# A two-layer hybrid trunk on one core: attention's query blocks first to last, values block by block, output projection in another order, squares summed on ScalarE

## The chip, the core and the metric

The kernel runs on one core of a Trainium2 chip. The core has TensorE (PE in the profile; PEld is its loading of weights), VectorE (DVE), ScalarE (ACT), GpSimd (POOL) and SyncE (SP), which issues most DMA transfers. Each engine works through its own list of instructions in order; semaphores hold an instruction until what it needs is there. Matmuls write to PSUM, eight banks of 128 x 512 floats; all else lies in SBUF. The metric is the time of one execution on the device in microseconds (us).

## The reference: what is computed

The input is one sequence of 512 tokens of width 1024, float32. Two layers follow one another, each of them:

```python
x = x + 0.5 * swiglu(rms_norm(x, ffn1_norm[l]), ...)            # d_ff 2816
h = rms_norm(x, mix_norm[l])
a, g, q, k, v = jnp.split(h @ w_in[l], splits, axis=-1)          # each 512 wide
conv_out = conv_module(a, g, ...)     # a * sigmoid(g), causal depthwise conv of 31 taps, RMSNorm, SiLU
diff_out = diff_attention(q, k, v, ...)
x = x + jnp.concatenate([conv_out, diff_out], axis=-1) @ w_out[l]
x = x + 0.5 * swiglu(rms_norm(x, ffn2_norm[l]), ...)
```

The differential attention has 4 heads. Of each head two causal softmax maps are made (keys of width 64, with a relative-position bias); the first minus lambda times the second multiplies the values of width 128. The result of each head is normalised by its root mean square over the 128 values of a token.

## The kernel before

The activations lie transposed, features on partitions and tokens along the row: `x` is 8 tiles of 128 x 512. Large products are done as three matmuls of a high and a low part (`mm3`, lines 159, 162 and 163): high by high, low by high, high by low. The parts of the weights are made on the chip: `chunk` (line 99) loads 128 x 1024 floats by a DMA on SP's queue, ScalarE makes the high part (line 96), and VectorE or GpSimd subtracts to get the low part (line 97). These tiles come from rings: five raw buffers, four for high and four for low parts, and a buffer is given back when its last reader is done.

A layer is a feed-forward block, the mixer and another feed-forward block. The change touches the mixer alone (function `mixer`, lines 526 to 815). Its work in program order:

- `conv_in` projects the convolution's input in four channel groups; `project` gives q and k for two pairs of token blocks of 128, `to_features` transposes them to features (`qz`, `kt`). q and k of blocks 0 and 1 come in the first pair.
- `project_values(j)` gives the values of token block j: 24 matmuls of 512 columns into a bank with the tag "mm", then a copy with a scale (line 614).
- `conv_taps(c, n)` does the 31 taps of channel group c. Group 0 is done on GpSimd (products by ScalarE, line 652, sums by GpSimd, line 653), groups 1 and 2 on VectorE in a PSUM bank (lines 660 and 665), group 3 with ten taps on GpSimd and 21 on VectorE. `conv_finish` gathers the statistics, spreads them over the partitions (`rcv`), and makes the four finished tiles `ch`, `cl` (lines 675 to 684).
- Attention runs in 16 steps, a query block i of 128 tokens and a head h each. `softmaxes` makes the scores of both maps in a bank of the tag "sc" and one of "po" (two banks each), adds the bias and finds the row's extremum (line 703), takes the exponential with a row sum (line 707), and combines the maps (lines 710 to 713). `keys_first` transposes the combined map and copies it, `values` multiplies by the values into a bank of "mm" (`pos[i]`), and after head 3 of a block normalises all four heads at once: square on ScalarE (738), sum on VectorE (740), power on GpSimd (`rsqrt`), product on VectorE (744). `block_out` transposes the block back and writes its high and low parts into `ch`, `cl` (lines 756 to 761). The row of a step grows with the block: block i has (i + 1) x 128 keys. `attend(n)` issues the softmax of step n, the transposes of step n - 2, the values of n - 3 and, where a block is complete, its output at n - 5.
- The output projection takes 4 tiles of the conv half (`half` 0) or of the attention half (`half` 1) for each of 8 output tiles; its products go to banks of "sc" and "po" in turn and are added to `x` by VectorE (line 810). It ends with `after(m)`, which makes the next block's input parts and squares (`Prep.tile`, lines 249 to 260).

Before the change attention takes the last query block first. The value projections stand between the first two steps, all conv taps before the third. The three passes of the output projection are the conv half for all tokens, the attention half for the last 256 tokens and the attention half for the first 256 tokens. The last two use the same weight chunks, which are loaded once for both.

Program order is not the order on the engines. The kernel is written in a framework with a planner, which simulates the program with costs of its own (`schedule_with_timeline_sim=True`, line 912): whenever an engine comes free in that simulation, the planner takes the earliest instruction in program order whose inputs and buffers are ready. The list of each engine is then fixed; on the chip an instruction that comes late holds up those behind it. Only where the code says `keep_in_program_order` is an order kept; none of these places is touched.

Of the kernel before, what the change touches and what calls it, by code (L numbers as in the profile page):

```python
# [11 lines left out]
F32 = mybir.dt.float32  # L12
F32R = mybir.dt.float32r
I32 = mybir.dt.int32
AF = mybir.ActivationFunctionType
ALU = mybir.AluOpType
AX = mybir.AxisListType

P = 128
DEPTH = 2  # L20
SEQ = 512
DM = 1024
KT = DM // P
NT = SEQ // P
# [4 lines left out]
CT = CC // P  # L29
TAPS = 31  # L30
PAD = TAPS - 1
HEADS = 4
HD = 64
VD = 2 * HD
# [14 lines left out]
POOL_TAPS = (TAPS, 0, 0, 10)  # L49
# [17 lines left out]
def trunk(ctx: ExitStack, tc: tile.TileContext, xt, par, lamv, relb, onehot,  # L67
          gu1, dn1, wag, wqkv, wout, gu2, dn2, out):
    nc = tc.nc
    V, S, G, T = nc.vector, nc.scalar, nc.gpsimd, nc.tensor  # L70

    const = ctx.enter_context(tc.tile_pool(name="const", bufs=1))
    small = ctx.enter_context(tc.tile_pool(name="small", bufs=2))
    act = ctx.enter_context(tc.tile_pool(name="act", bufs=1))
    wp = ctx.enter_context(tc.tile_pool(name="wp", bufs=1))
    tmp = ctx.enter_context(tc.tile_pool(name="tmp", bufs=2))
# [3 lines left out]
    def f32(ap):  # L80
        return ap.bitcast(F32)
# [3 lines left out]
    def bank(tag, name):  # L85
        return psum.tile([P, 512], F32, tag=tag, name=name, bufs=BANKS[tag])
# [12 lines left out]
    def chunk(src, eng=None):  # L99
        raw, hi, lo = ring("wraw"), ring("whi"), ring("wlo")  # L100
        nc.sync.dma_start(raw, src)
        parts_of(raw, hi, lo, eng)
        return hi, lo
# [74 lines left out]
    for half in range(2):  # L178
        h, kk = slice(half * 512, (half + 1) * 512), range(half * KT // 2, (half + 1) * KT // 2)
# [21 lines left out]
    def rsqrt(v, n, use=""):  # L201
        y = small.tile([P, n], F32, tag=f"rs_y{n}{use}", name="rs_y")
        G.tensor_tensor(y, v, mhalf[:, :n], op=ALU.pow)
        return y
# [60 lines left out]
    def wpart(w, b, n=P):  # L265
        return w[0][:, b * n : (b + 1) * n], w[1][:, b * n : (b + 1) * n]
# [223 lines left out]
    nlam, gq, gsub, ghalf = [], [], [], []  # L490
# [35 lines left out]
    def mixer(l, pr, after):  # L526
        with tc.tile_pool(name="mix", bufs=1) as mp, tc.tile_pool(name="mt", bufs=2) as mt:
# [74 lines left out]
            def project_values(j):  # L602

                if 2 not in wts:
                    wts[2] = [chunk(wqkv[l, 2, kc], G) for kc in range(KT // 2)]
                t = slice(j * P, (j + 1) * P)
                ps = bank("mm", "ps_v")
                for k in range(KT):
                    wh, wl = wpart(wts[2][k // 2], k % 2, 512)
                    xh, xl = pr[k]  # L610
                    T.matmul(ps, xh[:, t], wh, start=k == 0, stop=False)  # L611
                    T.matmul(ps, xh[:, t], wl, start=False, stop=False)
                    T.matmul(ps, xl[:, t], wh, start=False, stop=k == KT - 1)
                S.activation(vv[:, j].rearrange("p h d -> p (h d)"), ps, AF.Copy, scale=row["c"][:, j : j + 1])
# [59 lines left out]
            def conv_finish():  # L674
                rcv = spread(rows_rstd(csum, CC, "c")[0], "rb")
                for c in range(CT):
                    z = ys[c]
                    hg = ghalf[l][:, c : c + 1]
                    G.tensor_tensor(z, z, rcv, op=ALU.mult)
                    th = mt.tile([P, SEQ], F32, tag="gl", name="th", bufs=1)  # L680
                    S.activation(th, z, AF.Tanh, scale=hg)
                    V.scalar_tensor_tensor(z, th, 1.0, z, op0=ALU.add, op1=ALU.mult)
                    S.activation(ch[:, c, :], z, AF.Copy, scale=hg)
                    V.scalar_tensor_tensor(cl[:, c, :], z, hg, f32(ch[:, c, :]), op0=ALU.mult, op1=ALU.subtract)


            steps = [(i, h) for i in reversed(range(NT)) for h in range(HEADS)]
            sums, pos, maps, ats = {}, {}, {}, {}

            def softmaxes(i, h):  # L690
                W = (i + 1) * P
                tq = slice(i * P, W)
                if h == 0:
                    sums[i] = small.tile([P, 2, HEADS], F32, tag="sums", name="sums")
                scs = [bank(tag, "ps_sc")[:, :W] for tag in ("sc", "po")]
                e0 = mt.tile([P, SEQ], F32, tag="e0", name="e", bufs=4)[:, :W]
                sm = sums[i]
                for m in range(2):
                    T.matmul(scs[m], qz[:, m, h, tq], kt[:, h, :W], start=True, stop=True)  # L699

                for m, (sc, e) in enumerate(zip(scs, (e0, scs[1]))):
                    mn = small.tile([P, 1], F32, tag=f"mn{m}", name="mn")
                    V.tensor_tensor_reduce(
                        out=e, in0=sc, in1=row["bias"][:, h, SEQ - W :], scale=1.0, scalar=3e38,
                        op0=ALU.add, op1=ALU.min, accum_out=mn,
                    )
                    S.activation(e, e, AF.Exp, bias=mn, scale=-1.0, accum_out=sm[:, m, h : h + 1])

                r2 = small.tile([P, 1], F32, tag="r2", name="r2")
                V.reciprocal(r2, sm[:, 1, h : h + 1])  # L710
                c2 = small.tile([P, 1], F32, tag="c2", name="c2")
                V.tensor_scalar(c2, r2, nlam[l], sm[:, 0, h : h + 1], op0=ALU.mult, op1=ALU.mult)
                V.scalar_tensor_tensor(e0, scs[1], c2, e0, op0=ALU.mult, op1=ALU.add)
                maps[i, h] = e0

# [9 lines left out]
            def values(i, h):  # L725
                if h == 0:
                    pos[i] = bank("mm", "ps_o")
                for j in range(i + 1):
                    T.matmul(pos[i][:, h * VD : (h + 1) * VD], ats[i, h][:, j * P : (j + 1) * P], vv[:, j, h, :],
                             start=j == 0, stop=j == i)  # L730
                if h < HEADS - 1:
                    return
                po = pos[i]

                se = small.tile([P, HEADS], F32, tag="se", name="se")
                V.scalar_tensor_tensor(se, sums[i][:, 0, :], VD * EPS, sums[i][:, 0, :], op0=ALU.mult, op1=ALU.mult)
                sq = tmp.tile([P, SEQ], F32, tag="sq", name="sq")
                S.activation(sq, po, AF.Square)
                so = small.tile([P, HEADS], F32, tag="so", name="so")
                V.tensor_reduce(so, sq.rearrange("p (h d) -> p h d", h=HEADS), axis=AX.X, op=ALU.add)  # L740
                G.tensor_tensor(so, so, se, op=ALU.add)
                ro = rsqrt(so, HEADS)
                ov = mt.tile([P, HEADS, VD], F32, tag="ov", name="ov")
                V.tensor_tensor(
                    ov, po.rearrange("p (h d) -> p h d", h=HEADS),
                    ro.unsqueeze(2).broadcast_to([P, HEADS, VD]), op=ALU.mult,
                )
                outs[i] = ov
# [14 lines left out]
            def attend(n):  # L763
                if n < len(steps):
                    softmaxes(*steps[n])
                if 2 <= n < len(steps) + 2:
                    keys_first(*steps[n - 2])
                if 3 <= n < len(steps) + 3:
                    values(*steps[n - 3])
                if n >= 5 and steps[n - 5][1] == HEADS - 1:  # L770
                    block_out(steps[n - 5][0])
# [14 lines left out]
            row["bias"] = bias  # L786

            for n in range(2):
                attend(n)
                project_values(NT - 1 - 2 * n)  # L790
                project_values(NT - 2 - 2 * n)
            for c in range(CT):
                conv_taps(c, POOL_TAPS[c])
            for n in range(2, len(steps) + 5):
                attend(n)
            conv_finish()

            for half, t in ((0, slice(0, SEQ)), (1, slice(SEQ // 2, SEQ)), (1, slice(0, SEQ // 2))):  # L800
                if t.stop == SEQ:
                    w = [None] * 4
                for m in range(KT):
                    if w[m // 2] is None:
                        w[m // 2] = chunk(wout[l, half, m // 2], G)
                    ps = bank(("sc", "po")[m % 2], "ps_out")[:, : t.stop - t.start]
                    for kk in range(4):
                        k = half * 4 + kk
                        mm3(ps, wpart(w[m // 2], (m % 2) * 4 + kk), (ch[:, k, t], cl[:, k, t]), kk == 0, kk == 3)
                    V.tensor_tensor(x[:, m, t], ps, x[:, m, t], op=ALU.add)  # L810

                    if half == 1 and t.start == 0 and m < KT // 2:
                        after(m)
            for m in range(KT // 2, KT):
                after(m)
# [101 lines left out]
```

## Time and profile before

| | us |
|---|---|
| median of 3 runs | 1803.87 (1802.54 to 1804.24) |
| the profiled execution | 1804.31 |
| its span, first to last instruction | 1802.2 |
| busy: TensorE, VectorE, ScalarE, GpSimd | 1785.8, 1202.8, 880.0, 624.4 |
| first layer's mixer in the trace, about | 376 to 560 |
| second layer's mixer, about | 1268 to 1452 |

Times of the trace count from its first instruction. A line of a group names the line of the code, the engine, the operation, what it writes and reads, the shape and how often; then the busy time, the mean of one in ns, and the idle time of its engine before it with what ended it. A row of the windows gives for a stretch of time how long each engine was busy in it, with the number of instructions, then the clock granted to TensorE, the share of the DMA engines and their rate. A row of waits says which instruction of an engine waited for which, how long in total, how often, and the longest. Matmuls overlap, and their recorded length is longer than the distance from one start to the next; an engine that shows as busy may still run below its best.

### The profile page before, as it was taken

How to read it: one execution, taken by the hardware profiler on the slowest of the kernel's cores; microseconds unless marked ns; L12 is line 12 of the kernel's file. 1: busy time of each engine (PE TensorE's matmuls, PEld its weight loads, DVE VectorE, ACT ScalarE, POOL GpSimd, SP SyncE). 2: the span in 40 equal slices, each digit the busy share in tenths (PEclk: the TensorE clock that was granted, in tenths of full speed). 3: DMA queues.
4: the chain of work that ended last, by engine and by line, in shares of the span. 5: the costliest groups of instructions: out<-in, count | busy, mean ns of one | idle time of the engine just before them, and what ended most of it. 6: DMA issues, size and time to landing. Idle time of an engine off the chain costs nothing.

```text
span 1802.2 us, 27871 instructions
## 1 busy us (share of the span) xinstructions
PE 1785.8 (99%) x10692; PEld 1584.9 (88%) x10692; DVE 1202.8 (67%) x1854; ACT 880.0 (49%) x1448; POOL 624.4 (35%) x430
## 2 busy tenths in 40 slices
PE   8999999999999999999999999999999999999999
PEld 6799899888778889899888998998887888998997
DVE  6957556568867857557576674665788587574662
ACT  5446345445854436346434462554558354463551
POOL 3025123269942024133110331322797320241320
PEclk9999999999999999999999999999999999999999
DMA  6446456333212346556433564664231133564561
GB/s 232 117 128 190 137 146 180 115 107 93 72 43 86 109 114 174 165 125 184 125 94 104 137 193 106 169 171 129 71 108 57 47 103 97 146 177 134 152 169 54
DMA packets 106021, 228.05 MB, mean 127 GB/s; under 512 B 11575, under 2 KB 29254, under 8 KB 105888
## 3 DMA queue, kind: packets, MB, share of 16 engines
q1 hardware_dynamic: 86880, 190.88, 32.7%
q0 software_dynamic: 18720, 35.23, 11.9%
q8 instruction: 83, 1.36, 0.3%
q14 instruction: 50, 0.41, 0.1%
q10 hardware_dynamic: 288, 0.16, 0.0%
HBM read 224.12 MB, written 3.42 MB: 126 GB/s over the span
## 4 chain that ended last, share of the span: by engine, by line
PE 95%; DVE 2%; issue 1%; ACT 1%; ACTq 0%; DVEq 0%
PE ps_pair L369 36%; PE ps_d L159 9%; PE ps_d L163 9%; PE ps_d L162 9%; PE ps_pair L162 6%; PE ps_pair L163 6%; PE ps_pair L159 6%; PE ps_pair L581 2%; PE ps_pair L583 2%; PE ps_pair L582 2%; PE ps_out L159 1%; PE ps_out L162 1%; PE ps_sc L699 1%; PE ps_out L163 1%; DVE actl L252 1%; PE ps_v L611 1%
## 5 line engine op out<-in xcount | busy, mean ns | idle before, releaser
L96 ACT ACTIVATE whi<-wraw 128x512 fp32r<-128x512 f32 (+1 forms) x580 | 458.0, 813 | 656.4 <-PE ps_d L162 226.3
L97 DVE TENSOR_TENSOR wlo<-wraw,whi 128x512 fp32r<-128x512 f32 (+1 forms) x536 | 509.5, 973 | 191.3 <-ACT whi L96 186.8
L369 PE MATMUL ps_pair<-acth,wlo 128*128 128x256 f32 x1024 | 289.8, 283 | 0.0
L369 PE MATMUL ps_pair<-actl,whi 128*128 128x256 f32 x1024 | 289.8, 283 | 0.0
L369 PE MATMUL ps_pair<-acth,whi 128*128 128x256 f32 x1024 | 289.7, 283 | 0.0
L162 PE MATMUL ps_d<-hl,whi 128*128 128x512 f32 x704 | 274.0, 389 | 0.0
L163 PE MATMUL ps_d<-hh,wlo 128*128 128x512 f32 x704 | 272.7, 389 | 0.0
L159 PE MATMUL ps_d<-hh,whi 128*128 128x512 f32 x704 | 268.7, 389 | 0.0
L137 POOL DMA_DIRECT2D wraw<-in_gu x64 | 77.2, 1206 | 464.5 <-DMA wraw<-in_gu 239.5
L369 PE MATMUL ps_pair<-th,wlo 128*128 128x256 f32 x768 | 217.3, 283 | 0.0
L369 PE MATMUL ps_pair<-tl,whi 128*128 128x256 f32 x768 | 217.2, 283 | 0.0
L369 PE MATMUL ps_pair<-th,whi 128*128 128x256 f32 x768 | 217.2, 283 | 0.0
L159 PE MATMUL ps_pair<-acth,whi 128*128 128x512 f32 x512 | 201.4, 396 | 7.6 <-ACT whi L96 7.6
L162 PE MATMUL ps_pair<-actl,whi 128*128 128x512 f32 x512 | 200.6, 393 | 0.7 <-DVE actl L252 0.6
L163 PE MATMUL ps_pair<-acth,wlo 128*128 128x512 f32 x512 | 200.2, 392 | 0.0
L142 POOL TENSOR_TENSOR wraw<-wraw 128x512 f32<-128x512 f32 x64 | 89.0, 1391 | 314.0 <-DMA wraw<-in_gu 268.9
L369 PEld LDWEIGHTS ps_pair<-actl,whi 128*128 128x128 f32 x1024 | 196.6, 192 | 0.3
L369 PEld LDWEIGHTS ps_pair<-acth,whi 128*128 128x128 f32 x1024 | 196.6, 192 | 0.3
L369 PEld LDWEIGHTS ps_pair<-acth,wlo 128*128 128x128 f32 x1024 | 196.6, 192 | 0.0
L465 DVE SCALAR_TENSOR_TENSOR x<-ps_d,x 128x512 f32<-128x512 f32 x96 | 64.9, 688 | 196.4 <-PE ps_d L163 196.4
L163 PEld LDWEIGHTS ps_d<-hh,wlo 128*128 128x128 f32 x704 | 132.2, 188 | 27.0
L159 PEld LDWEIGHTS ps_d<-hh,whi 128*128 128x128 f32 x704 | 132.2, 188 | 26.9
(171 smaller groups left out, 3308.1 us busy)
## 6 DMA issues: line engine op xcount, KB each, us to landing
wraw<-in_gu SPq DMA_DIRECT2D x108, 512.0 KB, 3.7
wraw<-in_gu SPq DMA_DIRECT2D x200, 256.0 KB, 4.0
wraw<-in_gu POOLq DMA_DIRECT2D x64, 512.0 KB, 5.8
wraw<-in_wqkv SPq DMA_DIRECT2D x24, 512.0 KB, 3.6
wraw<-in_dn SPq DMA_DIRECT2D x52, 192.0 KB, 3.1
wraw<-in_wag SPq DMA_DIRECT2D x16, 512.0 KB, 3.5
wraw<-in_wout SPq DMA_DIRECT2D x16, 512.0 KB, 3.5
wraw<-in_dn SPq DMA_DIRECT2D x24, 320.0 KB, 3.4
```

What stands on the lines that cost most here:

```text
L96: S.activation(hi, raw, AF.Copy)
L97: (eng or V).tensor_tensor(out=lo, in0=raw, in1=f32(hi), op=ALU.subtract)
L137: nc.gpsimd.dma_start(two.rearrange("p (b c) -> p b c", b=2), u[:, h[0]].unsqueeze(1).broadcast_to([P, 2, 512]), accum_op=ALU.add)
L142: G.tensor_tensor(more[:, h[0]], two[:, h[1]], whole[:, h[0]], op=ALU.add)
L159: first = T.matmul(ps, wh, xh, start=start, stop=False)
L162: T.matmul(ps, wh, xl, start=False, stop=False)
L163: T.matmul(ps, wl, xh, start=False, stop=stop)
L369: mm = T.matmul(ps, l, r, start=first and i == j == 0, stop=False, skip_group_check=True)
L465: V.scalar_tensor_tensor(x[:, m, :], ps, 0.5, x[:, m, :], op0=ALU.mult, op1=ALU.add)
L581: T.matmul(ps[n], xh[:, t], wh, start=k == 0, stop=False)
L582: T.matmul(ps[n], xh[:, t], wl, start=False, stop=False)
L583: T.matmul(ps[n], xl[:, t], wh, start=False, stop=k == KT - 1)
```

## The change

- The steps of attention go through the query blocks 0, 1, 2, 3 instead of 3, 2, 1, 0.
- The value projection of block 0 stands before the first step, that of block 1 before the second, that of block 2 before step 3 and that of block 3 before step 5.
- The taps of conv groups 0, 1 and 2 stay before step 2; those of group 3 go before step 8.
- The squares of the attention output are taken head by head, right after a head's values: an ACTIVATE on 128 x 128 with a row sum (`accum_out`). The square of the whole block and the sum on VectorE go.
- The coefficient c2 is made by a scalar_tensor_tensor in place of a tensor_scalar with two pointer operands.
- The output projection does the attention half for the first 256 tokens, then `conv_finish` and the conv half for all tokens, then the attention half for the last 256 tokens. Each pass loads its own four weight chunks, so a layer has twelve chunk loads there in place of eight.

```diff
-            steps = [(i, h) for i in reversed(range(NT)) for h in range(HEADS)]
-            sums, pos, maps, ats = {}, {}, {}, {}
+            steps = [(i, h) for i in range(NT) for h in range(HEADS)]
+            sums, pos, maps, ats, sos, squares = {}, {}, {}, {}, {}, {}
...
-                V.tensor_scalar(c2, r2, nlam[l], sm[:, 0, h : h + 1], op0=ALU.mult, op1=ALU.mult)
+                V.scalar_tensor_tensor(c2, r2, nlam[l], sm[:, 0, h : h + 1], op0=ALU.mult, op1=ALU.mult)
...
                 if h == 0:
                     pos[i] = bank("mm", "ps_o")
+                    sos[i] = small.tile([P, HEADS], F32, tag="so", name="so")
...
+                po, so, d = pos[i], sos[i], slice(h * VD, (h + 1) * VD)
+                if h == 0:
+                    squares[i] = tmp.tile([P, SEQ], F32, tag="sq", name="sq")
+                S.activation(squares[i][:, d], po[:, d], AF.Square, accum_out=so[:, h : h + 1])
                 if h < HEADS - 1:
                     return
-                po = pos[i]
...
-                sq = tmp.tile([P, SEQ], F32, tag="sq", name="sq")
-                S.activation(sq, po, AF.Square)
-                so = small.tile([P, HEADS], F32, tag="so", name="so")
-                V.tensor_reduce(so, sq.rearrange("p (h d) -> p h d", h=HEADS), axis=AX.X, op=ALU.add)
...
             for n in range(2):
+                project_values(n)
                 attend(n)
-                project_values(NT - 1 - 2 * n)
-                project_values(NT - 2 - 2 * n)
-            for c in range(CT):
+            for c in range(CT - 1):
                 conv_taps(c, POOL_TAPS[c])
             for n in range(2, len(steps) + 5):
+                if n == 8:
+                    conv_taps(CT - 1, POOL_TAPS[CT - 1])
+                if n in (3, 5):
+                    project_values((n + 1) // 2)
                 attend(n)
-            conv_finish()
...
-            for half, t in ((0, slice(0, SEQ)), (1, slice(SEQ // 2, SEQ)), (1, slice(0, SEQ // 2))):
-                if t.stop == SEQ:
-                    w = [None] * 4
+            for half, t in ((1, slice(0, SEQ // 2)), (0, slice(0, SEQ)), (1, slice(SEQ // 2, SEQ))):
+                if half == 0:
+                    conv_finish()
+                w = [None] * 4
...
-                    if half == 1 and t.start == 0 and m < KT // 2:
+                    if half == 1 and t.start and m < KT // 2:
                         after(m)
```

## The prediction

> **What bounds the kernel now.** First the page's table of busy time and its chain, then the windows over the mixer, then who makes TensorE wait there, then TensorE's own order of time.
>
> ```profile
> PE 1785.8 (99%) x10692; PEld 1584.9 (88%) x10692; DVE 1202.8 (67%) x1854; ACT 880.0 (49%) x1448; POOL 624.4 (35%) x430
> ...
> PE 95%; DVE 2%; issue 1%; ACT 1%; ACTq 0%; DVEq 0%
> ```
>
> TensorE (PE) is the bound of the whole program: no edit to another engine can pay more than the time in which PE now stands still. So the question is only where PE is starved.
>
> ```profile
> core 0: us, PE busy (x) PEld busy (x) DVE busy (x) ACT busy (x) POOL busy (x), PEclk, DMA share, GB/s
> 376.00:490.00 114.00, 114.00 (x520) 91.41 (x519) 92.04 (x159) 72.96 (x119) 106.31 (x64) 1.00 0.29 90
> 490.00:516.00 26.00, 23.77 (x146) 18.66 (x145) 25.25 (x91) 21.73 (x65) 12.36 (x13) 1.00 0.02 5
> 516.00:535.00 19.00, 19.00 (x90) 15.66 (x89) 8.04 (x15) 5.33 (x10) 8.35 (x5) 1.00 0.25 71
> ```
>
> In the first layer's mixer PE is full except in the 26 us in which attention ends and the conv half is finished; there VectorE (DVE) is 97% busy and ScalarE (ACT) 84%. The second layer's mixer is the same stretch 892.4 us later (23.78 busy of 26). Who ends PE's waits between 480 and 575 us, and the order in time at the worst place:
>
> ```profile
> PE ps_out L159 <- ACT acth L683: 1.3, 1, 1.3
> PE ps_at L720 <- ACT at L722: 0.4, 1, 0.4
> PE ps_o L729 <- ACT at L722: 0.2, 1, 0.2
> ```
>
> ```profile
> 504.99 0.73 PE L699 MATMUL ps_sc<-kt,qz 128*128 128x128 f32 x4
> 505.56 0.38 PE L720 MATMUL ps_at<-ident,e 128*128 128x128 f32 x2
> 507.20 0.50 PE L159 MATMUL ps_out<-acth,whi 128*128 128x512 f32 x1 [1.26 <-ACT acth L683]
> 507.54 0.45 PE L699 MATMUL ps_sc<-kt,qz 128*128 128x128 f32 x2
> 508.08 0.44 PE L720 MATMUL ps_at<-ident,e 128*128 128x128 f32 x2
> ```
>
> What the reader is to see: PE waits for the conv half (L683 is in conv_finish), because the first matmuls of the output projection are the conv half's and nothing else is left to run beside the short steps of the last blocks.
>
> The idle column understates the loss, since a matmul that starts late still counts as busy. I price the stretch by spacing from start to start: 0.111 us for a 128-wide value, transpose or score piece, 0.217, 0.323 and 0.43 for score pieces of 256, 384 and 512, 0.227 for a 512-wide and 0.120 for a 256-wide projection matmul (all read off back-to-back rows in time order). The stretch 490 to 516 holds 51 values, 22 + 12 + 4 transposes and 16 scores of 128 (105 x 0.111 = 11.7), 16 scores of 256 (3.5), 4 of 384 (1.3), 19 projection matmuls (4.3) and 2 of the spread (0.9): 21.7 us of work in 26. So 4.3 us are lost per layer, 2.2 of it shown as idle; 8.6 us in both. That is the most the change can win.
>
> **The change part by part.**
>
> *Output projection in another order.* Its three passes are 96 matmuls each: 96 x 0.120 = 11.5 us for either half of the tokens, 96 x 0.227 = 21.8 us for the conv half. PE work is the same in sum; what changes is what has to be ready. Work that PE can do from 455 us on without the conv half: value projection 96 x 0.227 = 21.8; scores 16 pieces of each width, 16 x (0.43 + 0.323 + 0.217 + 0.111) = 17.3; values 80 x 0.111 = 8.9; transposes (40 + 16) x 0.111 = 6.2; statistics and spread 1.3: 55.5 us. Now the conv half must be there after that; in the new order 11.5 us of first tokens come before it: 67.0 us.
>
> *What the other engines must do by then.* The windows from 455 to 516 us add up to 53.8 us of DVE, 50.5 of ACT and 45.6 of POOL. With a PE demand of 55.5 and dependences between them DVE can't keep up without gaps: that is the loss. The change alters their sums so, per layer:
> - DVE: four reduces less (0.678 each, 2.7); the 16 tensor_scalar with two pointer operands (0.269) become scalar_tensor_tensor, priced by the 128x4 one of L736 (0.152): 1.9 less; the first pass's eight 256-wide additions come earlier (8 x 0.42 = 3.4 more before the conv half). 53.8 - 4.6 + 3.4 = 52.6.
> - ACT: four squares of 128x512 less (0.595 each, 2.4); 16 squares of 128x128 from PSUM more. No such row exists; the nearest, the 128x128 copy from PSUM of L722, took 0.274, and an accumulator read as in L707 takes 0.200, half of it beside the next instruction. So 16 x 0.274 = 4.4 to 16 x 0.474 = 7.6; I take 0.374, 6.0, as those rows overlap so. Four more weight casts (L96, 1.058) 4.2. 50.5 - 2.4 + 6.0 + 4.2 = 58.3.
> - POOL: four more subtractions for the weights' low parts (2.394): 9.6. 45.6 + 9.6 = 55.2.
>
> All three now lie 8 us or more under PE's 67.0, where DVE was 1.7 under. PE should be the longest sum again in this stretch.
>
> *Blocks first to last, value projection block by block.* Scores of blocks 0 and 1 need the first 256 tokens of q and k alone, ready when the copies at 449.3 to 451.7 us end, against 459.9 for the last ones; the first scores now start at 463.6. So ACT (which stands idle 3.7, 1.9 and 1.3 us between 442 and 457) and DVE can start up to 10 us sooner. PE fills with value projections, of which only the first two stand ahead of attention. I book no gain beyond the filled gaps: PE is full before 490 us anyway. What is queued behind: ps_o and ps_v share the two "mm" banks, so pos[0] and value projections 2 and 3 take turns; the bank frees after one copy of 0.69 us (L614), covered by scores.
>
> *POOL and SP queues.* The last conv channel's ten POOL taps (1.29 each) now rank behind eight steps of attention. Of 114 us before 490, POOL is busy 106, so a cast that the planner puts ahead of them is late by 2.4 each; now already four casts (475.4 to 487.3 us) stand between those taps, which end at 491.3, and the first pass's four take that very place. The four casts of the next pass come only as its chunks fall free, one per 2.9 us. On SP's queue four more 512 KB loads per layer pass (3.5 us to landing; the DMA share in the stretch is 0.02); the next feed-forward's gate and up loads stand behind them, yet its casts (550.0 us on) wait for slots that the last pass frees at the same pace in both versions. I book nothing; the cover is the 22 us of the conv pass.
>
> *Tail.* The last pass now needs block 3 instead of block 1. From its last score on, one step, squares, rsqrt (1.1), ov (0.68), transposes and the two copies take about 0.7 x 5 + 0.6 + 0.9 + 0.5 + 1.3 + 0.7 + 0.5 + 1.4 = 9.4 us; the conv pass of 21.8 us covers it.
>
> *Sum.* Of 4.3 us per layer I leave 1.0: the two waits for L722 (0.6) stay, since a transpose behind a copy is still in every step, and some late starts. 2 x 3.3 = 6.6 less. The profiled execution took 1804.31 us (span 1802.2 and 2.1 around it), 0.44 over the median; 1804.31 - 6.6 = 1797.7, or **1797.3** against the median.
>
> **The rivals.**
> 1. *The filler can't get in: no change.* The projection's ps_out takes the "sc" and "po" banks, two each, which two steps of attention fill. A step holds "po" from its score to L713, some 5 us. Eight accumulations of about 3 us need four turns of "po", so either they wait or attention slows by 4 x 3 / 2 = 6 us. For: in the trace only the last steps share banks with ps_out. Against: attention is then no longer what PE waits for. If nothing is filled and only DVE's 4.6 us shorten the stretch by a fifth or so, PE gains 1 us per layer: 1802.
> 2. *Block 3 ends last: slower.* If the planner sends the conv pass early, between blocks 2 and 3, the last pass stands behind block 3's chain with no cover: up to 9.4 us per layer, less the 4.3 saved, x 2: 1814. It decides when block 3's last score starts less than 9.4 us before the conv pass ends. Against: program order, which ranks attention ahead of all passes.
> 3. *POOL's casts ahead of conv_finish: slower.* If four casts stand ahead of POOL's taps or multiplications by rcv, the conv half is 9.6 us later; now 4.3 us are lost with 11.5 us less to fill, so this loses only if the filler is not ready either; then 9.6 - 4.3 = 5.3 per layer at most, and half of that likely: 1809. DVE work beside POOL grows too: L682 took 1.29 us beside a POOL multiplication and 0.68 with POOL idle.
> 4. *One long wait instead of many short.* At the start, behind idle times of 5.6 and 2.0 us, the first eleven matmuls stand 0.43 us apart until 13.8 us and 0.227 after it: 2.2 us lost. In the mixer the longest wait is 1.26 and no slower spacing follows. If rival 2's wait comes in one piece, each layer adds 2.2: 1818. The Trainium skill ("TensorE: Matmul & The Clock Gate", section "Why this matters for your kernels") says the same as a rule: no gaps of PE over some 3 us between bursts, or the array falls back to half rate. By that rule, too, only a wait longer than any of this mixer would cost; the slow start agrees with it, though the granted clock in the window rows reads 1.00 there.
>
> **How the numbers follow.** A gain of 6.6 us in 1804 is 0.37%. A measurement tells about 0.2%, 3.6 us, from no change. Forecast 0.63; rival 1 0.17; rival 2 0.08; rival 3 0.09; rival 4 0.03. Faster 0.63, same 0.17, slower 0.20. Low end: all 8.6 us gone, 1795, and the late starts at 560 to 570, where matmuls worth 9.5 us fill 10 in either layer: 1794. High end: rival 3's 1809, which leaves rivals 2 and 4 out. The forecast's own range is 1794 to 1800.
>
> **What would show it.** Right: PE idle in the 26 us before the conv half under 1 us; 256-wide ps_out matmuls between the scores of blocks 2 and 3; no PE wait for L683; the DVE groups of L740 gone and c's near 0.15; squares of 128x128 near 0.3 us. Wrong: a PE wait for L758 or L759 ahead of the last pass (rival 2); conv taps on POOL ending after 500 us with casts before them (rival 3); first-token ps_out starting only after the last scores (rival 1). The forecast fails if the planner's order, which I can't see, has PE stand behind a step that on the chip is later than planned.

## The result and the profile after

The changed kernel took 1808.72 us (median; 1808.42 to 1809.05) against 1804.05 us (1801.98 to 1804.68) for the kernel before on the same chip: a ratio of 1.0027, 95% interval 1.0017 to 1.0038. It is slower by 4.7 us, where 6.6 us less were forecast; 1808.7 lies just inside the range that was given. The profiled execution has a span of 1806.9 us.

Busy time and the chain that ended last, from the page of the changed kernel:

```profile
PE 1786.1 (99%) x10692; PEld 1583.6 (88%) x10692; DVE 1220.4 (68%) x1846; ACT 892.9 (49%) x1512; POOL 635.1 (35%) x438
...
PE 91%; DVE 5%; ACT 2%; issue 1%; DVEq 0%
```

TensorE did the same work, but the chain's share of VectorE rose from 2% to 5%. VectorE was to be relieved, and it is busy 17.6 us longer. The same stretch of the first layer's mixer, in windows (columns as in the prediction):

```profile
core 0: us, PE busy (x) PEld busy (x) DVE busy (x) ACT busy (x) POOL busy (x), PEclk, DMA share, GB/s
455.00:480.00 25.00, 25.00 (x126) 20.84 (x126) 23.28 (x60) 21.38 (x49) 23.18 (x18) 1.00 0.17 51
480.00:490.00 10.00, 6.91 (x27) 3.65 (x27) 8.30 (x24) 7.10 (x30) 10.00 (x8) 1.00 0.58 185
490.00:500.00 10.00, 8.92 (x45) 5.61 (x44) 9.84 (x27) 8.51 (x28) 3.78 (x5) 1.00 0.02 5
500.00:510.00 10.00, 10.00 (x65) 7.83 (x64) 9.85 (x28) 7.86 (x25) 3.83 (x4) 1.00 0.00 0
510.00:520.00 10.00, 9.91 (x74) 8.53 (x73) 9.88 (x23) 7.77 (x18) 4.76 (x5) 1.00 0.01 2
```

The reader is to see a hole that has moved. Before, TensorE was full until 490 us and short of work from there on. Now 500 to 520 is filled, as forecast, and the hole lies at 480 to 490: 6.91 busy of 10, beside a GpSimd (POOL) that never stops; the ten us behind it lack another 1.1. Who makes TensorE wait there (470 to 530 us), and two of these waits in order of time:

```profile
PE ps_sc L699 <- DVE e L713: 2.1, 2, 1.7
PE ps_sc L699 <- DVE mn L703: 1.2, 2, 0.9
PE ps_o L756 <- DVE ov L744: 0.6, 1, 0.6
```

```profile
484.22 0.70 PE L699 MATMUL ps_sc<-kt,qz 128*128 128x256 f32 x2 [1.68 <-DVE e L713]
...
487.71 2.58 PE L699 MATMUL ps_sc<-kt,qz 128*128 128x384 f32 x6 [0.91 <-DVE mn L703]
```

The wait for L683 is gone. In its place scores wait for score banks that VectorE frees late. Priced from start to start with the durations of the prediction, in pieces of 10 us from 460 to 520 us (pieces that lose less than 0.35 left out), TensorE loses about 5.1 us in the first layer before and 7.2 us after; in the second layer 5.0 and 6.9. The prediction's own 26 us gave 4.3 for before; the pieces are used below to compare kernels.

What holds VectorE is above all one line. The groups of the coefficient c2 (L712) and of se, between 440 and 560 us of the changed kernel, and the durations of c2 (minimum, median, maximum in ns) over the whole execution; then, in a fence of its own, those of c2 and se before. se is the small term (row sums squared, times a constant) that is added to a block's sums of squares; its line is L740 in the changed kernel and L736 before, where L740 was the reduce.

```profile
L712 DVE SCALAR_TENSOR_TENSOR c<-r,nlam,sums 128x1 f32<-128x1 f32 x16 | 10.5, 656 | 0.2
L740 DVE SCALAR_TENSOR_TENSOR se<-sums 128x4 f32<-128x4 f32 x4 | 2.6, 661 | 0.0
...
L712 DVE SCALAR_TENSOR_TENSOR c<-r,nlam,sums x32: 204/410/2103, 463.7 to 1412.9; 128x1 f32<-128x1 f32 x32
```

```profile
L712 DVE TENSOR_SCALAR c<-r,nlam,sums x32: 259/268/275, 469.9 to 1410.0; 128x1 f32<-128x1 f32 x32
...
L736 DVE SCALAR_TENSOR_TENSOR se<-sums x8: 133/155/171, 483.6 to 1403.9; 128x4 f32<-128x4 f32 x8
```

An operation on one element per partition takes up to 2.1 us. In order of time, VectorE first, then GpSimd:

```profile
475.69 2.10 DVE L712 SCALAR_TENSOR_TENSOR c<-r,nlam,sums 128x1 f32<-128x1 f32 x1
...
482.02 1.62 DVE L712 SCALAR_TENSOR_TENSOR c<-r,nlam,sums 128x1 f32<-128x1 f32 x1
...
485.64 1.54 DVE L740 SCALAR_TENSOR_TENSOR se<-sums 128x4 f32<-128x4 f32 x1
...
488.59 0.22 DVE L712 SCALAR_TENSOR_TENSOR c<-r,nlam,sums 128x1 f32<-128x1 f32 x1
```

```profile
475.36 2.42 POOL L97 TENSOR_TENSOR wlo<-wraw,whi 128x1024 fp32r<-128x1024 f32 x1
...
478.96 4.66 POOL L97 TENSOR_TENSOR wlo<-wraw,whi 128x1024 fp32r<-128x1024 f32 x2
...
484.82 2.35 POOL L97 TENSOR_TENSOR wlo<-wraw,whi 128x1024 fp32r<-128x1024 f32 x1
...
488.51 1.00 POOL L203 TENSOR_TENSOR rs_y<-so,mhalf 128x4 f32<-128x4 f32 x1
```

The c2 that starts at 475.69 ends at 477.79, and the subtraction that GpSimd has running ends at 477.78 (475.36 + 2.42). The next ends at 483.64, GpSimd's at 483.62; se ends at 487.18, GpSimd's at 487.17. So the small VectorE operation ends when the running GpSimd operation does. At 488.59 GpSimd works on 128x4, and c2 takes 0.22. Of the layer's sixteen c2, eight stand still so: they take 8.77 us instead of 8 x 0.21 = 1.7, 7.1 us too much; two of the four se take 2.3 us instead of 0.3, 2.0 too much.

### The profile page after: what moved, and what is told of

The parts are those of the page before. It is cut to its first block, busy times and chain, and to the rows that moved or that the text cites. A ratio compares the mean times of both kernels' runs of the same rounds, so it can differ in the third digit from the quotient of the medians.

```text
span 1806.9 us, 27977 instructions
## 1 busy us (share of the span) xinstructions
PE 1786.1 (99%) x10692; PEld 1583.6 (88%) x10692; DVE 1220.4 (68%) x1846; ACT 892.9 (49%) x1512; POOL 635.1 (35%) x438
## 4 chain that ended last, share of the span: by engine, by line
PE 91%; DVE 5%; ACT 2%; issue 1%; DVEq 0%
PE ps_pair L369 36%; PE ps_d L159 9%; PE ps_d L163 9%; PE ps_d L162 9%; PE ps_pair L162 6%; PE ps_pair L163 6%; PE ps_pair L159 6%; PE ps_pair L582 2%; PE ps_pair L581 2%; PE ps_pair L583 2%; PE ps_out L163 1%; PE ps_out L159 1%; PE ps_out L162 1%; DVE actl L252 1%; DVE c L712 1%
## 5 line engine op out<-in xcount | busy, mean ns | idle before, releaser
L96 ACT ACTIVATE whi<-wraw 128x1024 fp32r<-128x1024 f32 (+1 forms) x588 | 466.9, 817 | 675.1 <-PE ps_d L162 226.3
```

The lines of the kernel that those rows point to most:

```text
L96: S.activation(hi, raw, AF.Copy)
```

## The experiments

Theory P: an operation of VectorE whose two tensor inputs both lie in SBUF (c2 in its new form reads r2 and sums, se reads sums twice) stands still until GpSimd's running two-input instruction ends; that is the loss. Rival O: the new order makes the hole at 480, and the long c2 only fill a VectorE that has nothing else to do. Four kernels took c2 and the order apart.

**The change without its c2.**

```diff
-                V.scalar_tensor_tensor(c2, r2, nlam[l], sm[:, 0, h : h + 1], op0=ALU.mult, op1=ALU.mult)
+                V.tensor_scalar(c2, r2, nlam[l], sm[:, 0, h : h + 1], op0=ALU.mult, op1=ALU.mult)
```

> The changed kernel with c2 made by tensor_scalar again; all else of the change stays. Theory P (the new c2 has two tensor inputs in SBUF and stands still until a running two-input instruction of GpSimd ends): c2 goes back to 0.27 us each, VectorE saves about 7 us per layer between 460 and 510 us, and TensorE loses some 2 us per layer in place of 7; time 1797 to 1801 us. Theory O (the new order itself is slower: nothing to fill in is ready before 505 us): the time stays above 1806 us whatever c2 takes.

Measured: 1803.14 us (1802.52 to 1804.19), ratio to before 0.9996 (0.9988 to 1.0005). One line is 5.6 us of the changed kernel's time. But the rest of the change then brings nothing, and the time is 2 us above the range of theory P: P accounts for the loss, not for the gain that never came. The windows of this kernel:

```profile
480.00:490.00 10.00, 9.05 (x41) 5.36 (x42) 8.25 (x30) 9.29 (x37) 10.00 (x8) 1.00 0.56 177
490.00:500.00 10.00, 9.89 (x50) 6.23 (x49) 9.48 (x31) 8.64 (x29) 4.65 (x5) 1.00 0.03 10
500.00:510.00 10.00, 10.00 (x66) 7.89 (x65) 9.00 (x23) 6.13 (x18) 5.66 (x5) 1.00 0.00 0
510.00:520.00 10.00, 9.26 (x78) 8.83 (x78) 8.97 (x20) 9.17 (x21) 3.11 (x4) 1.00 0.01 2
```

The hole at 480 is smaller but there. Priced, it is 2.8 us at 480, 0.7 at 490 and 1.3 at 510: 4.8 us, as much as before the change in another place.

**The new c2 alone, in the kernel before.** The same edit the other way round.

> The kernel before with the new c2 alone. Theory P: in the old order about half of the 16 c2 of a layer begin beside a two-input instruction of GpSimd; with what was left of these in the trace of before they wait 3 to 4 us per layer in sum, 1 us is saved on the others; time 2 to 5 us above before, 1806 to 1809 us. Theory O: a shorter instruction, no loss; 1803 to 1804 us.

Measured: 1804.96 us (1802.72 to 1805.93), ratio 1.0006 (0.9997 to 1.0015): no clear difference, between the two expectations. Its c2 took 0.203, 0.220 and 0.667 us (minimum, median, maximum). In the first layer seven of the 16 still end within 0.02 us of GpSimd's running instruction, but none began with more than 0.67 us of it left, and in sum they wait 1.6 us where theory P had put 3 to 4. The price of the instruction depends on what lies beside it.

**The order alone.** The change (blocks, value projections, conv taps and passes) with c2 and the squares as before; two places of its edit:

```diff
-            steps = [(i, h) for i in reversed(range(NT)) for h in range(HEADS)]
+            steps = [(i, h) for i in range(NT) for h in range(HEADS)]
...
-            for half, t in ((0, slice(0, SEQ)), (1, slice(SEQ // 2, SEQ)), (1, slice(0, SEQ // 2))):
+            for half, t in ((1, slice(0, SEQ // 2)), (0, slice(0, SEQ)), (1, slice(SEQ // 2, SEQ))):
```

> The new order of blocks, value projections, conv taps and passes alone: c2 and the squares as before the change. Theory P: like the run with c2 undone, 1797 to 1802 us, VectorE 2.7 us per layer busier by the sums. Theory O: at or above 1806 us.

Measured: 1803.44 us (1802.71 to 1803.81), ratio 0.9999 (0.9990 to 1.0008), between what P and O had expected. With the old squares the order by itself neither wins nor loses.

**One input of c2 in PSUM.** The change with the reciprocal written into a score bank that its step still owns, so that c2 has a single tensor input in SBUF.

```diff
-                r2 = small.tile([P, 1], F32, tag="r2", name="r2")
+                r2 = scs[0][:, :1]
```

> The changed kernel, but the reciprocal that c2 reads lies in PSUM, in the step's own score bank, so the same scalar_tensor_tensor has one tensor input in SBUF. Theory P: every c2 takes 0.2 to 0.3 us, also while GpSimd runs a two-input instruction, and the time falls toward 1798 to 1803 us (the score bank is held longer, which may cost some of it). If the wait has another cause (the operation or its tiny shape), c2 still takes up to 2 us and the time stays near 1809 us.

Measured: 1804.89 us (1804.50 to 1805.30), ratio 1.0007 (0.9998 to 1.0015), just above the range of theory P and 3.8 us under the changed kernel. Its c2 over the whole execution, one of them in order of time, and GpSimd at that moment:

```profile
L712 DVE SCALAR_TENSOR_TENSOR c<-ps_sc,nlam,sums x32: 203/214/219, 463.3 to 1405.5; 128x1 f32<-128x1 f32 x32
...
482.34 0.22 DVE L712 SCALAR_TENSOR_TENSOR c<-ps_sc,nlam,sums 128x1 f32<-128x1 f32 x1
```

```profile
478.28 4.67 POOL L97 TENSOR_TENSOR wlo<-wraw,whi 128x1024 fp32r<-128x1024 f32 x2
```

The same operation of VectorE, in the middle of the same subtraction of GpSimd (which ends at 482.95), takes 0.22 us, and the longest of all is 0.219 where it was 2.103. This shows the mechanism: it is where the inputs lie, not the operation nor the order. This form stays 1.8 us over the tensor_scalar, and why was not tested apart. The score bank is now held until c2 has read it, which costs a wait of its own; and se, still with both inputs in SBUF, takes 3.1 us in the first layer here against 2.2 beside the tensor_scalar. TensorE's waits, 470 to 530 us:

```profile
PE ps_sc L699 <- DVE c L712: 1.9, 2, 1.4
```

That settles what the new c2 costs. Open was why an order that fills 500 to 520 wins nothing. Theory F: the filler was only taken from elsewhere. The value projections, ranked ahead of steps 3 and 5, run in one piece until 477.5 us, and the first-token pass can't start before the output of block 1 is done (500.5 us; it starts at 502.1); between them stand short steps with nothing beside them. Rival G: the short steps are late for VectorE and ScalarE, whatever lies beside them.

**Value projections later.** The change with the old c2 and two numbers altered; then the same with a place between.

```diff
-                if n in (3, 5):
-                    project_values((n + 1) // 2)
+                if n in (7, 11):
+                    project_values((n + 1) // 4)
```

> The changed kernel with c2 as tensor_scalar again, and with the value projections of token blocks 2 and 3 moved later in program order, from ahead of steps 3 and 5 to ahead of steps 7 and 11. Theory F (the order moved the hole: with c2 put back, TensorE loses nothing between 500 and 510 us, but 2.8 us between 480 and 490, because value projections are used up by 477.5 and block 1's output, which the first-token pass needs, is not ready before 500): the 22 us of value projection now lie beside the short steps, so the loss at 480 to 490 falls from 2.8 to under 1 us a layer, the whole from 4.8 to some 3, and the time to about 1800 (1799 to 1801.5), a gain of 0.1 to 0.25% over the kernel before. Rival G (the short steps are late for DVE and ACT, whatever lies beside them, so a filler moved there only uncovers the place where it was taken from): 1802.5 to 1804, and the loss shows before 480.

Measured: 1808.43 us (1807.84 to 1809.06), ratio 1.0026 (1.0016 to 1.0036). Theory F in this form falls, and the time is above the range of G too. The hole at 480 did not close; it began at 460 (1.3, 2.3, 1.8 us at 460, 470, 480) and came back at 500 (2.2).

```diff
-                if n in (3, 5):
-                    project_values((n + 1) // 2)
+                if n in (5, 9):
+                    project_values((n + 3) // 4)
```

> The changed kernel with c2 as tensor_scalar again and the value projections of token blocks 2 and 3 ahead of steps 5 and 9 (the change has 3 and 5; with 7 and 11 the time was 1808.4 and TensorE lost 1.3, 2.3 and 1.8 us at 460, 470 and 480, and 2.2 at 500). If the place of the filler has a best point between (theory F in part): a loss at 480 to 490 below 2.0 us without a new one before 480, and 1800.5 to 1802.5. If each of these blocks only moves the hole, since VectorE and ScalarE set how fast the short steps go: 1803 to 1806.

Measured: 1811.89 us (1811.66 to 1813.32), ratio 1.0046 (1.0032 to 1.0060): worse still, and outside both expectations. Its windows:

```profile
455.00:470.00 15.00, 14.33 (x75) 11.77 (x74) 14.03 (x41) 12.28 (x34) 13.61 (x11) 1.00 0.23 71
470.00:480.00 10.00, 9.11 (x42) 6.47 (x40) 9.51 (x31) 8.95 (x29) 9.41 (x9) 1.00 0.00 1
480.00:490.00 10.00, 9.56 (x51) 6.86 (x51) 9.75 (x33) 9.32 (x33) 4.45 (x5) 1.00 0.01 2
490.00:500.00 10.00, 10.00 (x46) 7.02 (x45) 7.62 (x19) 8.40 (x19) 9.54 (x5) 1.00 0.35 106
500.00:510.00 10.00, 8.32 (x39) 5.68 (x38) 9.41 (x25) 8.80 (x26) 7.31 (x8) 0.90 0.34 104
```

From 455 to 490 VectorE is 94 to 98% busy (ScalarE 82 to 93%) while TensorE has gaps. By these rows the steps run as fast as VectorE lets them once the filler is out of the way, and that is too slow to feed TensorE; the filler then lies where TensorE needs none. That speaks for G, without showing it apart. The granted clock of 0.90 in the last row is a dip to 0.50 from 508 to 511 us, right behind a wait of 1.57 us for L713. It is not what makes this kernel slower: in the second layer the clock reads 1.00 over the same stretch, and TensorE loses as much there (about 9 us in either layer).

**The passes in the old order.** Blocks first to last, old c2, squares by head, but the conv half first; the two passes of the attention half then share one set of loaded weights, as before the change.

```diff
-            for half, t in ((1, slice(0, SEQ // 2)), (0, slice(0, SEQ)), (1, slice(SEQ // 2, SEQ))):
+            for half, t in ((0, slice(0, SEQ)), (1, slice(0, SEQ // 2)), (1, slice(SEQ // 2, SEQ))):
```

> The changed kernel with c2 as tensor_scalar again and the output projection's passes put back to conv half first (then first tokens, then last tokens, on one set of loaded weights); blocks still first to last, values block by block, squares by head. Theory F (the first-token pass does fill PE at 500 to 510): without that filler the stretch before the conv half is short of work again, now behind the hole at 480 to 490 that the block order makes; 2 to 4 us a layer more than with the first tokens first, so 1807 to 1811. Rival G (passes don't matter, since what is won at 500 is lost at 480 because the four weight casts of the first pass hold POOL and ACT there): the casts are those of the conv pass instead, as before the change, and the time is 1803 to 1804.

Measured: 1807.10 us (1806.32 to 1808.57), ratio 1.0019 (1.0010 to 1.0028), 4 us over the same kernel with the first tokens ahead. Here TensorE loses 2.7 us at 480, 0.4 at 490 and 3.4 at 500. So the first-token pass does what it was put there for: it takes away the 3.4, of which 1.3 come back at 510.

**The squares alone.** The kernel before with the squares by head and no reduce.

```diff
+                S.activation(squares[i][:, d], po[:, d], AF.Square, accum_out=so[:, h : h + 1])
...
-                sq = tmp.tile([P, SEQ], F32, tag="sq", name="sq")
-                S.activation(sq, po, AF.Square)
-                V.tensor_reduce(so, sq.rearrange("p (h d) -> p h d", h=HEADS), axis=AX.X, op=ALU.add)
```

> The kernel before with only the squares moved to ScalarE by head, with accumulated sums; no reduce on VectorE. VectorE has 2.7 us less a layer, ScalarE 3.6 us more. If VectorE's sum bounds the stretch before the conv half (97% busy there), 1 to 2 us a layer are won: 1800 to 1802. If dependences between the steps do, no change: 1803 to 1804.5. If ScalarE's longer work is what a step then waits for, 1805.

Measured: 1799.78 us (1798.74 to 1800.33), ratio 0.9977 (0.9969 to 0.9986): 4 us faster than before, and the fastest kernel here. The windows at the old hole, first before, then with this edit:

```profile
490.00:500.00 10.00, 9.37 (x63) 7.75 (x62) 9.46 (x33) 7.65 (x23) 4.72 (x5) 1.00 0.03 12
500.00:510.00 10.00, 8.57 (x55) 6.67 (x54) 9.79 (x41) 9.03 (x28) 6.43 (x6) 1.00 0.00 0
```

```profile
490.00:500.00 10.00, 10.00 (x68) 8.55 (x68) 9.70 (x34) 8.87 (x34) 4.33 (x5) 1.00 0.01 2
500.00:510.00 10.00, 9.04 (x57) 7.17 (x56) 9.36 (x43) 9.63 (x40) 6.04 (x6) 1.00 0.00 0
```

2.7 us less of VectorE per layer, and TensorE's loss is some 3.2 us instead of 5.1 in the first layer; the last score starts at 510.3 instead of 515.1 us. That speaks for VectorE as the limit of the stretch, which was 95 to 98% busy there. But the edit also shortens the chain at a block's end, where a square of 128x512 and the reduce stood behind the last values, and no run separates the two. In the new order the same edit brings 0.3 us (1803.44 without it, 1803.14 with it, both with the old c2), which is no difference. So the new order is not free once the squares are made by head: against this kernel it costs 7.3 us with the passes in the old order (1807.10), of which the first-token pass wins back 4.0.

**Squares by head for blocks 2 and 3 only.** To see why the squares win nothing in the new order: the change with the old c2, and with the old square and reduce for blocks 0 and 1.

```diff
+                if i < 2:
+                    sq = tmp.tile([P, SEQ], F32, tag="sq", name="sq")
+                    S.activation(sq, po, AF.Square)
+                    V.tensor_reduce(so, sq.rearrange("p (h d) -> p h d", h=HEADS), axis=AX.X, op=ALU.add)
```

> The changed kernel with c2 as tensor_scalar again, and the squares of blocks 0 and 1 as before the change (one square of 128x512 and a reduce on VectorE), those of blocks 2 and 3 by head on ScalarE. Theory A (in the new order ScalarE bounds the stretch 474 to 493 us, where it runs without a gap on four weight casts, conv products and the steps of blocks 0 and 1, so that the squares by head, which win 4 us in the old order, add there what they save VectorE later): TensorE's loss at 480 to 490 is that of the order alone (1.6 us a layer instead of 2.8) and at 490 to 500 that of the squares (0.7 instead of 1.9), 1.2 us a layer less than with either form for all blocks: 1800.5 to 1801.5. Rival B (the hole is there for lack of matmuls, whatever ScalarE does): 1803 to 1803.5, as with either form.

Measured: 1802.07 us (1801.21 to 1802.81), ratio 0.9991 (0.9982 to 1.0000), between theory A and rival B, and not to be told from the kernel with all squares by head. The trace shows half of A: the loss at 480 falls from 2.8 to 1.9 us, but at 490 it rises from 0.7 to 1.5. That speaks for a share of ScalarE in the hole, and again most of it moves on.

**se on ScalarE.** The change with the old c2, and the other operation with two inputs in SBUF made by ScalarE.

```diff
-                V.scalar_tensor_tensor(se, sums[i][:, 0, :], VD * EPS, sums[i][:, 0, :], op0=ALU.mult, op1=ALU.mult)
+                S.activation(se, sums[i][:, 0, :], AF.Square, scale=math.sqrt(VD * EPS))
```

> The changed kernel with c2 as tensor_scalar again and with se, the other scalar_tensor_tensor whose two tensor inputs lie in SBUF, made by a Square activation on ScalarE (128x4). With c2 back, se still takes VectorE 2.2 us a layer in four instructions (0.543 each) where 0.6 were planned. Theory P: these 1.6 us go; they sit beside GpSimd's running subtractions in 480 to 510, where TensorE waits, so 0.5 to 1.5 us a layer, 1800.5 to 1802.5. If four stalls are absorbed by the steps between: 1803.

Measured: 1802.05 us (1801.49 to 1803.27), ratio 0.9992 (0.9983 to 1.0001); se takes ScalarE 0.214 each. 1.1 us less than with se on VectorE, on the side that P expects, but within what the intervals leave open.

**The loads alone.** The kernel before with the third pass's weights loaded and cast again.

```diff
-                if t.stop == SEQ:
-                    w = [None] * 4
+                w = [None] * 4
```

> The kernel before with only the weights of the third pass of the output projection loaded and cast again instead of kept: four more loads of 512 KB, four casts of ScalarE (1.06 us) and four subtractions of GpSimd (2.4 us) a layer. As I booked it (hidden behind the conv pass, nothing): 1803 to 1804.5. If the later feed-forward's loads and casts behind them come late: 1 to 3 us more, 1805 to 1807.

Measured: 1803.71 us (1802.52 to 1808.42), ratio 1.0002 (0.9993 to 1.0011). Four loads, casts and subtractions more per layer cost nothing, as booked.

**The pass without the block order.** The squares alone, blocks last to first as before, and ahead of the conv half the attention half of the tokens that are then ready first.

```diff
-            for half, t in ((0, slice(0, SEQ)), (1, slice(SEQ // 2, SEQ)), (1, slice(0, SEQ // 2))):
-                if t.stop == SEQ:
-                    w = [None] * 4
+            for half, t in ((1, slice(SEQ // 2, SEQ)), (0, slice(0, SEQ)), (1, slice(0, SEQ // 2))):
+                if half == 0:
+                    conv_finish()
+                w = [None] * 4
```

> The kernel before with the squares by head, and the idea of the change's projection order without its block order: blocks still last to first, and ahead of the conv half the attention half of the tokens that are then ready first, the last 256; then the conv half, then the first 256 tokens; three sets of loaded weights. With the squares alone TensorE loses 2.4 us a layer at 500 to 510. If a pass that is ready there is filler in the old block order as well: the loss falls to under 1 us a layer and the time to 1795.5 to 1798. If the output of blocks 2 and 3 comes too late or its additions on VectorE delay the last steps: 1800, as with the squares alone, or up to 1803.

Measured: 1808.32 us (1806.28 to 1810.01), ratio 1.0025 (1.0015 to 1.0035): 8.5 us over the squares alone, and outside both expectations. The first matmul of that pass, and a second wait in the middle of it:

```profile
511.00 0.62 PE L159 MATMUL ps_out<-acth,whi 128*128 128x256 f32 x3 [0.67 <-ACT acth L758]
...
512.39 0.46 PE L730 MATMUL ps_o<-vv,at 128*128 128x128 f32 x2 [0.66 <-DVE actl L759]
```

The pass needs all of block 2, whose output comes off VectorE and ScalarE only near 511 us, later than the conv half that it was put ahead of (507 in the kernel before). A filler that waits for the same two engines is none: TensorE lost 4.4 us at 500 and 1.9 at 510. In the second layer it lost some 2 us more, and there the granted clock fell behind the waits:

```profile
1405.00:1410.00 5.00, 4.82 (x23) 4.47 (x22) 4.46 (x11) 2.82 (x8) 0.71 (x1) 0.50 0.00 2
```

Until 1411 us the 256-wide matmuls of the pass start 0.213 us apart, and 0.120 after that. The longest single wait ahead of it was 1.10 us.

## Why the prediction was wrong

- **The bound and the place (held).** TensorE is the bound of the whole, and what it lost lay in this stretch. The squares alone speak for VectorE as its limit there: 2.7 us a layer off VectorE, with a shorter chain at each block's end, won 4.1 us in two layers.
- **The c2 price (the step that failed, and the sign with it).** "the 16 tensor_scalar with two pointer operands (0.269) become scalar_tensor_tensor, priced by the 128x4 one of L736 (0.152): 1.9 less." They took 0.656: 10.5 us a layer where 2.4 were booked, and se 2.6 where 0.6 stood. VectorE's time from 455 to 516 us went from 53.8 to 57.2 us, where 52.6 were forecast; with the old c2 it is 53.7. The row was wrong because its eight instances of before (0.133 to 0.171) all ran with GpSimd idle or, twice, within 0.17 us of the end of its subtraction. The right row stood in the trace and in the prediction: L682, which also reads two tensors in SBUF, took 1.29 beside GpSimd's 128x512 multiplication L679 and 0.68 otherwise (the prediction says "with POOL idle"; one of the layer's three began beside the 128x4 power of L203). I used it for a rival's extra cost and not for the price of the form that the change was about to use sixteen times.
- **The sums of demand (failed second).** "All three now lie 8 us or more under PE's 67.0 ... PE should be the longest sum again in this stretch." TensorE's sum was the longest, as forecast. VectorE's was nearly right with the old c2 (53.7 over 455 to 516; 54.5 by the prediction with c2 at its old price), and ScalarE's and GpSimd's came out lower than 58.3 and 55.2 (50.7 and 45.4), since the extra casts came only from 517.7 us on and a square took less than booked. But such a sum says nothing of where in the stretch the work can lie. The prediction's "PE is full before 490 us anyway" was read off an order in which, from 478 us on, the longest steps stood (scores of 512 and 384). The new order has shorter steps there (256 and 384), behind value projections that were used up at 477.5. TensorE then lost 2.8 us at 480 to 490 where it had lost none, and the 6.6 us expected became 0: with the old c2 the ratio to before is 0.9996, and 0.9999 for the order alone. Why the steps there are late is not shown apart; the moved value projections speak for VectorE.
- **The filler itself (held).** 256-wide ps_out matmuls run from 505.5 us among the last scores (from 502.1 with the old c2), no PE wait for L683 is left, and 500 to 510 is full. The first-token pass is worth 4 us against the old order of the passes; the block order that it needs, with the squares by head, costs 7.3.
- **The squares (priced too high, and the worth was missed).** They take 278 ns each and the accumulator read about 0.2, but the two and the next instruction overlap: from the start of a square to the start of the next instruction, where ScalarE doesn't wait, it is 0.25 to 0.27 us nearly always, where 0.374 was taken. That they would win 4 us alone was not seen; rival 1 had put VectorE's whole relief at 1 us a layer.
- **Attention's start (held, as was booking no gain for it).** The first scores start at 457.3 instead of 463.6 us.
- **Loads, queues and tail (held).** The loads alone cost nothing that can be told (ratio 1.0002). TensorE is full from 520 to 560 us; no wait for L758 or L759 stands ahead of the last pass.
- **The rivals.** None named the cause. Rival 1's time, 1802, is near the change with the old c2, but not by its mechanism, since the filler got in. Rival 2 did not come: block 3 is covered. Rival 4 did not come in the profiled execution of the change, where the longest PE wait in the stretch is 1.68 us and the granted clock 1.00; in seven of the nine executions the mean clock reads 0.998 or 0.999, and these took at most 0.33 us longer than the other two. But its slower matmuls are real: two other kernels show a granted clock of 0.50 for 3 to 7 us behind waits of 1.57 and of 1.10 us at most. So the prediction's "only a wait longer than any of this mixer would cost" does not hold, the longest of before being 1.26; the length of one wait doesn't tell it, and what does is not shown. Rival 3 had GpSimd's subtractions in the right place (475 to 487 us) and the wrong victim: TensorE never waited for conv_finish, though GpSimd's first multiplication there came at 507.9 instead of 502.5 us; c2 stood still for them. Its 1809 stands beside 1808.7 by chance.

## What to carry to other kernels

Price a small VectorE instruction by its form and by what GpSimd is running beside it, not by its size: with two tensor inputs in SBUF its row must be taken at a moment when GpSimd is in a long operation. In these runs the tensor_scalar with pointer operands and the form with one input in PSUM never waited for GpSimd. A sum of demand over a stretch is only a lower bound; ask at each place of the new order which matmuls are ready there, and by which engine they become ready. When a change has several parts, take the part that relieves the limiting engine alone first: here it wins 4 us without the rest.

## What the runs showed that was not expected

VectorE's scalar_tensor_tensor with both tensor inputs in SBUF ended within 0.03 us of the end of GpSimd's running tensor_tensor of 128x512 or 128x1024, in each of the ten cases of the first layer in which it began 0.5 us or more before that end (0.60 to 2.10 us for work of 0.15 to 0.22). The same operation with one input in PSUM (0.203 to 0.219) and the tensor_scalar with two pointer operands (0.255 to 0.275) never stood still beside the same instructions. The Trainium skill ("SBUF — State Buffer", section "SBUF: two separate sides") says that VectorE and GpSimd share one pair of SBUF ports as an exclusive lock, that a VectorE operation with two SBUF inputs needs it against a GpSimd operation that reads SBUF, and that the loser stands still for the whole of the other's instruction. The traces agree for the large operations, to 0.03 us. They don't for GpSimd's 128x4 power of L203: c2 took 0.22 us at 488.59, inside that instruction's 1.00 us. How much of that time the power reads SBUF, no run shows.
